# Last attention rows of the sample kept in SBUF, and three more PSUM banks for the last output products

## The chip, the cores and the metric

The kernel runs on one core of a Trainium2 chip. The metric is the time of one execution on the device in microseconds (us); lower is better. Three runs of the kernel before gave a median of 1077.6 us (1075.97 to 1082.05). One further execution was profiled; its time and its span stand in the table below.

The core has a matrix engine (TensorE, PE in the profile; its weight loads are the row PEld), a vector engine (VectorE, DVE), an activation engine (ScalarE, ACT), a general engine (GpSimd, POOL) and SyncE (SP), on whose queue this kernel issues all its DMAs. SBUF is the on-chip memory that the engines read, PSUM the eight banks into which PE writes its products, and DRAM is off the chip.

## The reference, cut to what matters

One encoder layer is applied to a prompt of 1024 tokens and, with the same weights, to a sample of 512 tokens, 1024 channels each:

```
h = rmsnorm(x, norm_g);  z = h @ w_in
y_hy  = rmsnorm(x0 * long_conv(x1 * vv), on_hy) * silu(hy_gate)             # 512 channels
y_att = rmsnorm(neighbourhood_attention(q, k, v, rpb), on_att) * silu(att_gate)  # 512 channels
y     = x + concat([y_hy, y_att]) @ w_out                                   # 1024 -> 1024
```

Attention has 8 heads of 64 channels, so two heads fill 128 partitions; the kernel calls such two heads a pair, and the 512 attention channels are the four pairs 0 to 3. The RMS norm over all 512 attention channels needs the sum of squares of all four pairs.

## The kernel before, in words

Matrix products are done in split single precision. Each operand is a rounded part `hi` and a remainder `lo`, and a product is three matmuls: hi by hi, weight-lo by hi, weight-hi by lo.

The kernel is written as generators (`k_phase`, `hyena`, `attention`, `out_part`), which `weave` steps through in a planned order; the compiler's planner then orders the instructions of each engine, earlier program text first, some generators with a higher priority. Each engine works through its own instructions strictly in the order so fixed. A tile from a pool with a tag shares a fixed number of buffers with the other tiles of that tag; a new tile waits until an old one is released by its last reader.

**Attention of the sample** (`attention(Gs, ap)`, lines 877 to 1065). For each pair it loads q, k, v and a bias table, makes scores and softmax (`soft`, tag `sp`, two PSUM banks), and then the product with v (`values`, tag `tp`, three PSUM banks): two transposed blocks, each copied and split by ACT (line 1012) and DVE (line 1013), then a bank with the product, which ACT and DVE add into the SBUF tile `ya` (lines 1023, 1024). When a pair is done, `finish` (lines 1026 to 1037) squares `ya` (ACT), adds the squares into `sqs` (POOL), for the last pair starts the sum over channels on PE (`row_sum`, line 811), multiplies `ya` by the gate (DVE, line 1036, in the profile line 76), and writes it to the DRAM buffer `A_d`. `row_r` then makes the 1/RMS factor `ra_s` in fourteen small DVE instructions.

**Output** (`out_part`, lines 1068 to 1103). Part 0 is the hyena half of `w_out`, part 1 the attention half; a job is 512 tokens (two of the prompt, one of the sample). For its four blocks of 128 channels a job loads `A_d` into the tile `lo` (line 1078), ACT rounds it into `hi` (line 1079) and POOL subtracts (line 1080). Then, for each half h of the 1024 output columns and each t of four blocks of 128 tokens, one PSUM bank collects twelve matmuls: three for each block k of channels, in the order k = 0, 1, 2, 3. DVE scales the bank, adds it to `acc` (line 1100), and SP writes the result out (line 1102). In part 1 of the sample there are thus eight products P1 to P8 of twelve matmuls, 96 in all; block k is pair k, so the last three matmuls of every product need pair 3, and the scaling needs `ra_s`.

**Banks.** In this phase PSUM is divided into tags `mm` (2 banks), `mo` (1), `sp` (2) and `tp` (3). The products of the output take their banks from a fixed list (line 1209), which for P1 to P8 comes out as mm, mm, mo, mm, mm, mo, mm, mm. So three products can be open at a time.

The prompt's products and the sample's attention are woven together (line 1221); the sample's part 1 follows (line 1222).

Of the kernel before, what the change touches and what calls it, by code (L numbers as in the profile page):

```python
# [23 lines left out]
NB = 4  # L24
# [10 lines left out]
def f32(ap):  # L35
    return ap.bitcast(F32)


class Group:
    def __init__(self, name, L, x, out, z2, dec, tw0):  # L40
        self.name, self.L, self.x, self.out, self.z2, self.dec = name, L, x, out, z2, dec
        self.nt = L // P
        self.xs, self.hi, self.lo = [], [], []
        self.rows = L // GW
        self.B = 2 * L // P
        self.half = self.B // 2
        self.tw0 = tw0
        self.nseg = L // 512


class Kernel:
# [825 lines left out]
    def attention(self, G, ap):  # L877
        nc, v = self.nc, self.v
        L, nt, rows = G.L, G.nt, G.rows
        big = G.name == "p"  # L880
# [145 lines left out]
        def finish(pr, s, y):  # L1026
            sl = slice(s * 512, (s + 1) * 512)
            sq = sqs[:, sl] if pr == 0 else ap.tile([P, 512], F32, name="qkr", bufs=2)
            nc.scalar.activation(out=sq, in_=y, func=AF.Square)
            if pr:  # L1030
                self.add(sqs[:, sl], sqs[:, sl], sq, nc.gpsimd)
            if pr == NB - 1 and s == G.nseg - 1:
                self.row_sum(ssa, sqs, "sp")
            ga = ap.tile([P, 512], F32, name="qkr", bufs=2)
            self.dma(ga, self.ga_d[G.name][pr][:, sl])
            self.stt(y, y, v["on_att"][:, pr:pr + 1], ga, ALU.mult)
            self.dma(self.A_d[G.name][4 + pr][:, sl], y)

        pair, todo = load_pair(0)
        for f in todo:  # L1040
# [3 lines left out]
        for pr in range(NB):  # L1044
            nxt, todo = load_pair(pr + 1) if pr + 1 < NB else (None, [])
            for e in range(2):
                Vh = load_head(pr * 2 + e)
                for hf in range(2):
                    for unit in units:
                        ss = soft(pair, e, hf, unit)  # L1050
                        late = [(n - 1, f) for n, f in late]
                        for n, f in late:
                            if n == 0:
                                f()
                        late = [x for x in late if x[0] > 0]
                        late.append((1, lambda a=(pair, Vh, e, hf, unit, ss): values(*a)))
                        if e == 1 and hf == 1:
                            late.append((2, lambda a=(pr, unit[0], pair[3][unit[0]]): finish(*a)))
                        if e == 1 and todo:
                            todo.pop(0)()  # L1060
                        yield
            pair = nxt
# [5 lines left out]
    def out_part(self, part, jobs):  # L1068


        nc = self.nc
        for jb in jobs:
            G, sl = jb["G"], slice(jb["seg"] * 512, (jb["seg"] + 1) * 512)
            jb["hi"] = [jb["ops"].tile([P, 512], F32R, name=f"hi{k}") for k in range(4)]
            jb["lo"] = [jb["ops"].tile([P, 512], F32R, name=f"lo{k}") for k in range(4)]
            for k, (hi, lo) in enumerate(zip(jb["hi"], jb["lo"])):
                a = f32(lo)
                self.dma(a, self.A_d[G.name][part * 4 + k][:, sl])
                nc.scalar.copy(out=hi, in_=a)  # L1079
                self.sub(lo, a, f32(hi), nc.gpsimd)  # L1080
            if part == 0:
                jb["acc"] = jb["accs"].tile([P, 4, D], F32, name="acc")
        yield
        for h in range(2):
            hs = slice(h * 512, (h + 1) * 512)
            units = [self.take_w(("w_out", h, part, k // 2)) for k in range(4)]
            for jb in jobs:
                G, t0, acc = jb["G"], jb["seg"] * 4, jb["acc"]
                r = G.ratt if part else G.rhy
                if part == 0:  # L1090
                    self.dma(acc[:, :, hs], G.x[t0 * P:(t0 + 4) * P, hs].rearrange("(t p) c -> p t c", p=P))
                for t in range(4):
                    ps = self.bank(next(self.mm_tags))
                    tok = slice(t * P, (t + 1) * P)
                    for k, (whi, wlo) in enumerate(units):
                        hi, lo = jb["hi"][k][:, tok], jb["lo"][k][:, tok]
                        for i, (w, a) in enumerate(((whi, hi), (wlo, hi), (whi, lo))):
                            nc.tensor.matmul(ps, lhsT=a, rhs=w, start=(k == 0 and i == 0), stop=(k == 3 and i == 2))  # L1098
                    o = acc[:, t, hs]
                    self.stt(o, ps, r[:, t0 + t:t0 + t + 1], o)  # L1100
                    if part == 1:
                        self.dma(G.out[(t0 + t) * P:(t0 + t + 1) * P, hs], o)
                yield
# [11 lines left out]
    def run(self):  # L1115
# [16 lines left out]
        def cls(*cms):  # L1132
            for cm in cms:
                cm.__exit__(None, None, None)
# [84 lines left out]

        self.w_pools, self.w_bufs = itertools.cycle((wp, self.wp)), 8  # L1220
        self.weave(self.chain(self.out_part(0, jobs), self.out_part(1, jobs[:2])), self.attention(Gs, ap))
        self.weave(self.out_part(1, jobs[2:]))
        cls(wc, *cms[::-1], ac)
        self.psum("right")
# [149 lines left out]
```

## Time and profile before

| | |
|---|---|
| median of three runs | 1077.6 us |
| profiled execution, its own time | 1074.62 us |
| its span (first to last instruction) | 1072.8 us |
| granted clock of PE, mean over the span | 0.975 |
| PE busy | 996.7 us, 93% |
| DVE busy | 788.4 us, 73% |
| ACT busy | 455.0 us, 42% |
| POOL busy | 394.9 us, 37% |

The busy shares are means over stages with different limits. A granted clock of 1.00 is 2.4 GHz, of 0.50 is 1.2 GHz. Matmuls overlap, so the length of one is longer than the distance from its start to the next one's.

### The profile page before, as it was taken

Reading aid. Unit: us, or ns where it says so; the run is one execution under the profiler, and the core shown is the slowest. Engines: PE = TensorE matmul, PEld = TensorE weight load, DVE = VectorE, ACT = ScalarE, POOL = GpSimd, SP = SyncE. Lnnn points to the kernel's source line nnn. Section 1 sums busy time; section 2 is a strip of 40 time slices with the busy share of each in tenths; the row PEclk is TensorE's granted clock in tenths of the full one; section 3 lists DMA queues with packets and bytes.
Section 4 is the critical chain, followed back from the end, with each engine's and each line's share of the span. In section 5 each row is a group of like instructions: output and inputs, shape, how many; then the busy total and the mean of one; then the engine's idle time right before and its main releaser. Section 6 shows DMA issues by size and latency. Waiting matters only on the chain.

```text
span 1072.8 us, 16738 instructions
## 1 busy us (share of the span) xinstructions
PE 996.7 (93%) x5868; PEld 877.5 (82%) x5868; DVE 788.4 (73%) x2036; ACT 455.0 (42%) x942; POOL 394.9 (37%) x318
## 2 busy tenths in 40 slices
PE   3899899998999999999998999998999989999976
PEld 2889798887888888888886887888988878888765
DVE  5797949455148676977648999989878867867863
ACT  6543423332332322222216465565756652465530
POOL 1043221302133332424155534445355365654540
PEclk9999899999999999999999999999999989999998
DMA  8217261664721121211394343654654479445422
GB/s 304 70 40 232 100 222 62 211 209 143 249 65 52 69 67 55 82 39 64 111 302 119 104 116 105 174 138 130 182 152 126 122 245 307 139 142 161 132 92 98
DMA packets 105778, 148.46 MB, mean 138 GB/s; under 512 B 7665, under 2 KB 69947, under 8 KB 105183
## 3 DMA queue, kind: packets, MB, share of 16 engines
q1 hardware_dynamic: 105695, 147.40, 43.9%
q8 instruction: 46, 0.75, 0.3%
q14 instruction: 37, 0.30, 0.1%
HBM read 106.15 MB, written 41.22 MB: 137 GB/s over the span
## 4 chain that ended last, share of the span: by engine, by line
PE 59%; DVE 20%; DMA 11%; ACT 4%; issue 3%; SPq 1%; POOL 1%; DVEq 0%; ACTq 0%; POOLq 0%
PE bank L398 28%; PE bank L1098 9%; PE bank L411 4%; PE bank L450 4%; DMA dec<-in_dec_p_dram 3%; PE bank L1019 2%; PE bank L452 2%; PE bank L451 2%; PE bank L1010 2%; DVE zc L64 1%; DVE s_sb L988 1%; SPq L61 1%; DVE whi L371 1%; DMA K_s<-Kw 1%; DVE xk L64 1%
## 5 line engine op out<-in xcount | busy, mean ns | idle before, releaser
L64 POOL TENSOR_TENSOR wlo<-wraw,whi 128x512 fp32r<-128x512 f32 x150 | 222.0, 1486 | 483.9 <-ACT whi L371 341.3
L398 PE MATMUL bank<-hThi_p,whi 128*128 128x512 f32 x320 | 126.8, 396 | 3.8 <-DVE vg L64 3.8
L398 PE MATMUL bank<-hThi_p,wlo 128*128 128x512 f32 x320 | 126.8, 396 | 0.0
L398 PE MATMUL bank<-hTlo_p,whi 128*128 128x512 f32 x320 | 126.4, 395 | 0.0
L411 PE MATMUL bank<-whi,hThi_p 128*128 128x256 f32 x384 | 110.8, 290 | 4.9 <-ACT qsq L832 2.4
L411 PE MATMUL bank<-whi,hTlo_p 128*128 128x256 f32 x384 | 109.7, 291 | 0.0
L411 PE MATMUL bank<-wlo,hThi_p 128*128 128x256 f32 x384 | 109.3, 286 | 0.0
L992 ACT ACTIVATE s_sb<-s_sb,mx 128x360 f32<-128x360 f32 (+1 forms) x96 | 60.4, 630 | 75.7 <-DVE mx L988 74.9
L1098 PE MATMUL bank<-whi,hi 128*128 128x512 f32 x192 | 78.4, 410 | 6.4 <-ACT hi L1079 4.6
L411 PEld LDWEIGHTS bank<-whi,hThi_p 128*128 128x128 f32 x384 | 74.0, 193 | 7.1 <-ACT qsq L832 2.6
L1098 PE MATMUL bank<-wlo,hi 128*128 128x512 f32 x192 | 77.3, 403 | 0.0
L1098 PE MATMUL bank<-whi,lo 128*128 128x512 f32 x192 | 76.8, 404 | 0.0
L371 ACT CAST whi<-wraw 128x512 fp32r<-128x512 f32 x66 | 40.5, 620 | 81.5 <-PE bank L398 69.5
L411 PEld LDWEIGHTS bank<-wlo,hThi_p 128*128 128x128 f32 x384 | 74.1, 193 | 0.5 <-issue 0.5
L411 PEld LDWEIGHTS bank<-whi,hTlo_p 128*128 128x128 f32 x384 | 73.3, 193 | 0.5 <-issue 0.5
L398 PEld LDWEIGHTS bank<-hThi_p,whi 128*128 128x128 f32 x320 | 60.6, 189 | 15.9 <-DVE vg L64 4.0
L1019 PE MATMUL bank<-pt,V 120*64 120x256 f32 (+1 forms) x352 | 67.7, 299 | 4.5 <-DVE pt L64 2.5
L398 PEld LDWEIGHTS bank<-hThi_p,wlo 128*128 128x128 f32 x320 | 60.6, 189 | 12.1
L398 PEld LDWEIGHTS bank<-hTlo_p,whi 128*128 128x128 f32 x320 | 60.4, 189 | 12.0
L398 PE MATMUL bank<-hThi_s,whi 128*128 128x512 f32 x160 | 64.1, 403 | 3.8 <-ACT vg L832 3.2
L64 POOL TENSOR_TENSOR T<-cmask,qkr 128x480 f32<-128x480 f32 x32 | 39.5, 1242 | 67.4 <-DMA qkr<-in_rpb_dram 49.2
L64 DVE TENSOR_TENSOR pt<-bank,pt 120x384 fp32r<-120x384 f32 (+1 forms) x96 | 56.1, 595 | 11.0 <-ACT pt L1012 10.3
(276 smaller groups left out, 2692.9 us busy)
## 6 DMA issues: line engine op xcount, KB each, us to landing
wraw<-in_w_ch_dram SPq DMA_DIRECT2D x40, 512.0 KB
wraw<-in_w_tk_dram SPq DMA_DIRECT2D x24, 512.0 KB
V<-v_p SPq DMA_DIRECT2D x32, 240.0 KB
wraw<-in_w_out_dram SPq DMA_DIRECT2D x24, 256.0 KB
out_dram<-acc SPq DMA_DIRECT2D x24, 256.0 KB
v_p<-vg SPq DMA_DIRECT2D x32, 160.0 KB
K_p<-Kw SPq DMA_DIRECT2D x4, 1088.0 KB
x<-in_x_prompt_dram SPq DMA_DIRECT2D x8, 512.0 KB
```

Source lines behind the costliest of these rows:

```text
L61: eng.dma_start(out=out, in_=in_)
L64: (eng or self.nc.vector).tensor_tensor(out=out, in0=a, in1=b, op=op)
L371: next(self.w_round)(out=hi, in_=r)
L398: nc.tensor.matmul(ps, lhsT=w, rhs=h[s][:, k], start=(k == 0 and i == 0), stop=(k == KC - 1 and i == 2))
L411: nc.tensor.matmul(pss[t // 2][:, t % 2, :], lhsT=h[t // 4][:, k, t % 4 * P:(t % 4 + 1) * P], rhs=w, start=(k == 0 and i == 0 and t % 2 == ...
L450: mm(o, lhsT=c, rhs=z, start=True, stop=False)
L451: mm(o[:, 0:P], lhsT=ns if inverse else s, rhs=z[:, 1], start=False, stop=False)
L452: mm(o[:, P:], lhsT=s if inverse else ns, rhs=z[:, 0], start=False, stop=True)
L992: nc.scalar.activation(out=s_sb[:, :n], in_=s_sb[:, :n], func=AF.Exp, bias=mx, scale=-1.0, accum_out=l)
L1010: nc.tensor.transpose(out=tp_[0:120, c * P:(c + 1) * P], in_=s_sb[:, c * 120:(c + 1) * 120], identity=self.ident)
L1019: nc.tensor.matmul(o, lhsT=vl, rhs=pr_, start=(c == 0 and i == 0), stop=(c == ncu - 1 and i == 1))
L1098: nc.tensor.matmul(ps, lhsT=a, rhs=w, start=(k == 0 and i == 0), stop=(k == 3 and i == 2))
```

## The change

`finish` keeps the gated `ya` of the sample's last pair as `G.last` and does not write it to `A_d`. `out_part` makes `hi` and `lo` of the fourth block straight from that tile; the subtraction for this block runs on DVE (the default of `sub`), where POOL did it. And ahead of the sample's part 1 a new list of tags is set.

```diff
@@ Group.__init__
-        self.xs, self.hi, self.lo = [], [], []
+        self.xs, self.hi, self.lo, self.last = [], [], [], None
@@ attention / finish
-            self.dma(self.A_d[G.name][4 + pr][:, sl], y)
+            if pr == NB - 1 and not big:
+                G.last = y
+            else:
+                self.dma(self.A_d[G.name][4 + pr][:, sl], y)
@@ out_part
             for k, (hi, lo) in enumerate(zip(jb["hi"], jb["lo"])):
+                if part == 1 and k == 3 and G.last is not None:
+                    nc.scalar.copy(out=hi, in_=G.last)
+                    self.sub(lo, G.last, f32(hi))
+                    continue
@@ run
         self.weave(self.chain(self.out_part(0, jobs), self.out_part(1, jobs[:2])), self.attention(Gs, ap))
+        self.mm_tags = itertools.cycle(["mm", "mm", "mo", "tp", "tp", "tp"])
         self.weave(self.out_part(1, jobs[2:]))
```

P1 to P8 then take mm, mm, mo, tp, tp, tp, mm, mm: six banks before the first has to be used again.

## Rows read from the trace of the kernel before

**Rows 1.** The page's part 2: PE's busy tenths and the DMA rate in 40 slices.
```profile
PE   3899899998999999999998999998999989999976
...
GB/s 304 70 40 232 100 222 62 211 209 143 249 65 52 69 67 55 82 39 64 111 302 119 104 116 105 174 138 130 182 152 126 122 245 307 139 142 161 132 92 98
```

**Rows 2.** Chain of waits from 1000 us on: start us, length us, what (line).
```profile
1040.38 0.49 ACT pt L1012
...
1040.90 0.57 DVE pt L64
...
1041.51 0.81 PE bank L1019 x5
...
1042.34 0.37 ACT ya L1023
...
1042.74 0.44 DVE ya L64
...
1043.86 1.86 DVE ya L76
...
1045.74 1.99 DMA A_s<-ya
...
1047.75 2.55 DMA lo<-A_s
...
1050.33 0.62 ACT hi L1079
...
1051.00 3.36 PE bank L1098 x7
...
1054.38 0.76 DVE acc L76
...
1055.19 13.91 PE bank L1098 x60
...
1069.12 0.75 DVE acc L76
```

**Rows 3.** Busy time per stretch of the end: length, five engines (instructions), clock, DMA, GB/s.
```profile
1037.60:1042.30 4.70, 3.16 (x19) 2.15 (x18) 2.99 (x6) 1.32 (x3) 0.00 (x0) 1.00 0.01 3
1042.30:1051.00 8.70, 1.88 (x10) 1.79 (x9) 4.58 (x16) 1.61 (x3) 1.26 (x1) 0.60 0.20 60
1051.00:1055.20 4.20, 3.82 (x10) 2.71 (x10) 0.82 (x2) 0.00 (x0) 1.27 (x1) 0.62 0.00 0
1055.20:1069.10 13.90, 13.88 (x60) 11.17 (x60) 4.25 (x6) 0.00 (x0) 0.00 (x0) 1.00 0.36 132
1069.10:1072.80 3.70, 0.00 (x0) 0.00 (x0) 0.75 (x1) 0.00 (x0) 0.00 (x0) 0.79 0.19 71
```

**Rows 4.** The same view for one microsecond, where the clock fell.
```profile
1044.00:1045.00 1.00, 0.00 (x0) 0.00 (x0) 1.00 (x1) 0.00 (x0) 1.00 (x1) 0.50 0.00 0
```

**Rows 5.** PE in order of time: start, length, line, operation, count, idle before.
```profile
1037.25 0.39 PE L1098 MATMUL bank<-whi,lo 128*128 128x512 f32 x1
...
1039.80 0.49 PE L1010 MATMUL bank<-ident,s_sb 128*120 128x128 f32 x3
...
1045.22 1.87 PE L811 MATMUL bank<-ones,sqs 128*128 128x1 f32 x8 [2.92 <-POOL sqs L64]
```

**Rows 6.** POOL in order of time.
```profile
1031.60 5.78 POOL L64 TENSOR_TENSOR wlo<-wraw,whi 128x512 fp32r<-128x512 f32 x4
1043.90 1.26 POOL L64 TENSOR_TENSOR sqs<-sqs,qkr 128x512 f32<-128x512 f32 x1 [6.52 <-ACT qkr L1029]
1051.02 1.27 POOL L64 TENSOR_TENSOR lo<-lo,hi 128x512 fp32r<-128x512 f32 x1 [5.85 <-ACT hi L1079]
```

**Rows 7.** ACT in order of time: rounding of pair 2.
```profile
1029.07 0.62 ACT L1079 CAST hi<-lo 128x512 fp32r<-128x512 f32 x1 [0.41 <-DMA lo<-A_s]
```

**Rows 8.** DVE in order of time: the gate product of pair 2, the last step of `ra_s`.
```profile
1019.80 0.74 DVE L76 SCALAR_TENSOR_TENSOR ya<-ya,pc,qkr 128x512 f32<-128x512 f32 x1
...
1049.70 0.17 DVE L816 COPY ra_s<-rs_y 128x4 f32<-128x4 f32 x1
```

## The prediction

> **What bounds the kernel now.** I read the page's slices first: PE is busy nine tenths in nearly every slice, but only seven and six tenths in the last two [rows 1]. A loss that the mean of 93% hides sits at the very end. Next comes the chain of waits backwards from the last instruction [rows 2]. It shows the last output bank scaled at 1069.12, before it 60 matmuls of line 1098 without a hole, and before these a string in which PE does almost nothing: pair 3's last values are added into `ya`, gated, written to DRAM (1.99 us), read back (2.55), rounded by ACT (0.62), and only then multiplied. The stretches put a size on it [rows 3]. From 1037.6 to 1042.3 PE works 3.16 of 4.7 us on the last values; from 1042.3 to 1051.0 it works 1.88 of 8.7; from 1051.0 to 1055.2 it runs at a mean clock of 0.62; from 1055.2 on it is full.
>
> How much work waits there? Sixty matmuls start from 1055.19 [rows 2]: five whole products of twelve. So the first three products were open, each with the nine matmuls of k = 0 to 2 done (27, the last of them at 1037.25 [rows 5]) and the three of pair 3 missing, which are the nine matmuls of 1051.0 to 1055.2. That P4 did not go on at 1037.6 is a matter of banks: its k = 0 to 2 need `hi` of pair 2, rounded at 1029.07 [rows 7], and weights, whose last remainder was there at 1037.4 [rows 6]. Two limits therefore stand one behind the other, the way of pair 3 through DRAM and three open products; the change goes at both.
>
> **The change part by part.** All times are of the profiled execution (1074.62 us, span 1072.8), which is 3.0 us under the median of 1077.6; I carry the difference over to the median.
>
> *The way through DRAM.* The write and the read go, with the small issue gaps between: `ya` was final at 1045.72 (1043.86 + 1.86), the rounding began at 1050.33 [rows 2]. Now ACT, idle at that time, can begin at about 1045.74 and `hi` is there at 1046.4 instead of 1050.95: 4.6 us earlier. On SP's queue nothing stood behind these two issues but the output DMAs, which start after 1055, so the queue gives nothing else.
>
> *The remainder on DVE.* It was POOL's, 1.27 us [rows 6], and becomes a 128x512 DVE instruction with two SBUF inputs. Nearest rows: the gate product of pair 2 took 0.74 [rows 8], that of pair 3 took 1.86 [rows 2], beside POOL's addition from 1043.90 to 1045.16 [rows 6]. The new one would start at 1046.4, when POOL has nothing left, so I take 0.75 and keep 1.9 as the other end: `lo` at 1047.1 to 1048.3. Behind it on DVE stand the fourteen small instructions of `ra_s`, which ended at 1049.87 [rows 8] and now end up to 0.75 later, at 1050.6; who needs `ra_s` comes below.
>
> The page "SBUF — State Buffer" of the Trainium skill, section "Who interferes with whom", says that a DVE instruction with two SBUF inputs contends with a GpSimd instruction that reads SBUF. The 0.74 against 1.86 agrees. By that rule the move to DVE would cost the change its 1.1 us again if POOL were reading at 1046.4.
>
> *The banks.* The three `tp` banks serve the last `values`: one is free when the last block but one has been split, the next when the last has (1041.47), the third when `ya` has been added (1043.18) [rows 2]. So P4 can open at about 1041, P5 at 1041.5, P6 at 1043.2: 27 matmuls that PE can do while it waited. Price of one: 13.91 us for 60, 0.23 us [rows 2], so 6.2 us. I credit none of them to the holes before 1042.3, though P4 may find up to 0.7 us there.
>
> *The sum.* From 1042.3: 27 matmuls of k = 0 to 2, 6.2 us; in between the eight of `row_sum`, 1.87 us at the low clock they had [rows 5], 0.9 if at the full one; together to 1050.4 at the latest. By then `hi` and `lo` of pair 3 have been there for 2 us or more, so PE doesn't wait for them. Then the 18 last matmuls of P1 to P6, 4.1 us, to 1054.5; then P7 and P8, 24 matmuls, 5.5 us, to 1060.0. P7 needs a bank back, so P1 scaled: `ra_s` at 1050.6 plus 0.75 is 1051.4; if `row_sum` stands behind all 27, `ra_s` comes at 1050.4 + 2.8 + 0.75 = 1053.9, P1 is free at 1054.7, and P7 waits 0.2. PE's end was 1069.1, so 9.1 us are saved with every term at its dear end. With `row_sum` at the full clock (0.9) and P4 in the holes (0.7) it is 10.7. I take 9.5. The stretch behind PE's end, 3.7 us for the last scaling and its DMA [rows 3], stays: the eight output DMAs, 256 KB each, now follow each other in some 9 us, 233 GB/s, and slices of the page reach 304 and 307 [rows 1].
>
> Of these 9.5 us, some 1.6 come from the clock: 4.2 us at a mean of 0.62 [rows 3] hold 3.2 us at half speed, 1.6 us lost. PE before had next to no work between 1042.3 and 1051.0, and the clock was down to 0.50 by 1044 [rows 4]. With PE filled from 1041 I expect it to stay at 1.00.
>
> **The rivals.**
>
> *Clock down all the same.* For it: PE works only 3.16 of the 4.7 us before 1042.3 and part of this is transposes. Against it: throughout that stretch the clock was 1.00 [rows 3], and the fall came after 1.7 us with nothing at all. Price: one low stretch like that of 1051.0, 1.6 us, up to 3.2 if `row_sum` and the products are hit twice. Saved 6.3 to 7.9, so 1069.7 to 1071.3.
> The page "TensorE: Matmul & The Clock Gate" of the Trainium skill, section "Part 4: PE-mode transpose", says that transposes do not count as PE busy in the same way; by that rule the stretch to 1042.3 looks emptier to the gate than to the profile. The trace's 1.00 there doesn't bear it out so far.
>
> *Banks without use.* PE's order is fixed by the planner from its own durations. If it takes the gate product for 0.74 where the chip needs 1.86 [rows 2, 8], it may place the k = 3 matmuls, or `row_sum`, ahead of P5 and P6; PE then stands before a ready product. In the limit only the DRAM way counts: everything as before but 4.6 us earlier, 1073.0. For it: the planner let PE take k = 3 as soon as it saw `hi`. Against it: by program order and readiness 27 matmuls need 6.2 us, more than the 4.1 from 1042.3 to 1046.4, so at most P6 can fall behind, and costs a stall of about 1.5 us, which the range holds.
>
> *Slower: attention loses its banks.* P4 to P6 now draw on the tag that attention itself needs. P4 lacks only pair 2 long before the end, so the planner could open it, and at 1030 to 1037 also P5, in `tp` banks that then stay taken until pair 3 arrives. Attention would go through one bank: two blocks of 0.49 + 0.49 + 0.57 each, then about 0.8 + 0.4 + 0.4 for the product, 4.7 us a unit with nothing overlapped [rows 2, 5]. It decides from two units on (9.4 us, the whole gain); at three it is 1077.6 - 9.5 + 14.1 = 1082. Against it: attention has the higher priority, and PE was never without prompt products before 1037, so P4 would not have been called for.
>
> **How the numbers follow.** My forecast, 1077.6 - 9.5 = 1068, has a chance of 0.63 with its own range of 1065 to 1071 (the bounds 10.7 and 9.1, a stall of 1.5 and a little for the spread of the runs). More gain than that, because P4 and P5 fill holes before 1042: 0.06, about 1064. Clock down: 0.11, 1070.5. Banks without use: 0.14, 1073. Attention slowed: 0.06, 1082. The range from 1063 to 1074.5 leaves out the last and the tails. A measurement of this kernel tells 0.5% from no change, 5.4 us: faster means below 1072.2. The forecast, the greater gain and the clock case lie there, and a few of the third: 0.80. Same takes the rest of the third, 0.14; slower 0.06.
>
> **What would show it.** No DMA from `ya` and no read of A_s after the last gate product; ACT's rounding within 0.1 us behind it; some 27 matmuls of line 1098 between 1041 and 1050; a granted clock of 1.00 there; PE's last matmul near 1060 and one unbroken stretch of some 42 matmuls ahead of it; a span of about 1063. The step on banks is wrong if PE is still idle for more than 2 us between 1043 and the rounding's end; the forecast is wrong if the last values of attention end later than 1043.2, or if anything before 1037 has moved.

## The result and the profile after

The changed kernel has a median of 1065.79 us (1062.47 to 1069.32, four runs) beside 1078.01 us of the kernel before (1075.97 to 1082.05, four runs): ratio 0.9883, 95% interval 0.9838 to 0.9927. It is 12.2 us faster by the medians; 1068 was forecast. The profiled execution took 1062.47 us, its span is 1060.7 us. On another occasion the same kernel gave a ratio of 0.9916 (0.9891 to 0.9942); the two intervals overlap between 0.9891 and 0.9927.

Single runs of one kernel lie up to 15 us apart, and much of that arises ahead of the change. The last of the 27 matmuls that the first three products do without pair 3 started at 1037.25 in the trace before [rows 5], at 1035.73 in the one after, and at 1042.55 in a second trace of the same changed kernel; these last two executions are 6.8 us apart there and 6.8 us apart in their whole time. Up to that matmul PE's instructions stand in the same order in all traces of this document. So the traces are compared from its start on, which I call the *reference point*, and the time from there to the end of the span the *last stretch*: 1072.8 - 1037.25 = 35.55 us before, 1060.7 - 1035.73 = 24.97 after, 24.95 in the second trace. The change is worth 10.6 us by this measure. The kernel before was traced once; two kernels below that were traced twice differ between their traces by 0.3 and 2.5 us in the last stretch.

PE's slices on the page after: the last two now hold nine and eight tenths, where they held seven and six [rows 1].
```profile
span 1060.7 us, 16734 instructions
...
PE   3999899888999999999998898999999989999998
```
The chain of waits after, columns as in [rows 2]:
```profile
1037.72 0.74 PE bank L1019 x5
...
1039.41 0.39 PE bank L1019
1039.80 2.06 PE bank L1105 x9
1041.85 0.58 PE bank L1019 x5
1042.43 4.11 PE bank L1105 x18
1046.54 0.79 PE bank L811 x8
1047.33 9.70 PE bank L1105 x42
...
1057.05 0.75 DVE acc L76
```
Line 1105 is the old line 1098 (1102 or 1106 in some kernels below), and 1081 the rounding of the old line 1079 for pair 3. Before, this chain ran from `ya` over two DMAs and ACT to seven and then sixty matmuls [rows 2]. Now it doesn't leave PE from 1039.41 to 1057.03: nine matmuls of P4, the last value products, eighteen of P5 and P6, `row_sum`, then the 42 that were still to come. No DMA and no ACT is in it. Stretch by stretch (columns as in [rows 3]):
```profile
1036.10:1039.40 3.30, 1.98 (x13) 1.39 (x12) 2.44 (x6) 1.32 (x3) 0.00 (x0) 1.00 0.04 12
1039.40:1046.40 7.00, 6.99 (x34) 5.85 (x35) 2.86 (x3) 1.49 (x3) 1.29 (x1) 1.00 0.00 0
1046.40:1057.10 10.70, 10.61 (x51) 8.51 (x49) 7.75 (x23) 0.13 (x1) 0.00 (x0) 1.00 0.46 172
1057.10:1060.70 3.60, 0.00 (x0) 0.00 (x0) 0.70 (x1) 0.00 (x0) 0.00 (x0) 0.83 0.20 73
```
PE is busy 17.6 of 17.7 us at a clock of 1.00, where it had stretches at 0.60 and 0.62 [rows 3]. What is left at the end is the last scaling and its DMA, 3.6 us, as before.

PE in order of time, columns as in [rows 5]:
```profile
1035.73 0.39 PE L1105 MATMUL bank<-whi,lo 128*128 128x512 f32 x1
...
1042.27 0.40 PE L1105 MATMUL bank<-whi,hi 128*128 128x512 f32 x1
...
1046.38 0.95 PE L811 MATMUL bank<-ones,sqs 128*128 128x1 f32 x8
1047.19 0.49 PE L1105 MATMUL bank<-whi,hi 128*128 128x512 f32 x1
...
1050.05 1.52 PE L1105 MATMUL bank<-whi,lo 128*128 128x512 f32 x6
```
`row_sum` takes 0.95 us where it took 1.87 at the low clock. The first matmul with pair 3 is at 1047.19, the first with its remainder at 1050.05.

DVE after, in order of time: gate product, the new remainder, the end of `ra_s`.
```profile
1043.99 1.88 DVE L76 SCALAR_TENSOR_TENSOR ya<-ya,pc,qkr 128x512 f32<-128x512 f32 x1 [0.70 <-ACT qkr L1029]
1046.57 0.69 DVE L64 TENSOR_TENSOR lo<-ya,hi 128x512 fp32r<-128x512 f32 x1 [0.69 <-ACT hi L1081]
...
1049.95 0.17 DVE L816 COPY ra_s<-rs_y 128x4 f32<-128x4 f32 x1
```
ACT after, its last instruction:
```profile
1045.91 0.62 ACT L1081 CAST hi<-ya 128x512 fp32r<-128x512 f32 x1 [1.95 <-DVE ya L76]
```
The rounding follows the gate product (1045.87) after 0.04 us. It ends at 1046.53; PE wants it at 1047.19. That is a slack of 0.66 us, and it matters below.

### The profile page after: what moved, and what is told of

Same layout as the page of the kernel before. It is cut to its first block, busy times and chain, and to the rows that moved or that the text cites. A ratio compares the mean times of both kernels' runs of the same rounds, so it can differ in the third digit from the quotient of the medians.

```text
span 1060.7 us, 16734 instructions
## 1 busy us (share of the span) xinstructions
PE 991.3 (93%) x5868; PEld 871.3 (82%) x5868; DVE 788.5 (74%) x2037; ACT 455.1 (43%) x942; POOL 392.8 (37%) x317
## 4 chain that ended last, share of the span: by engine, by line
PE 53%; DVE 25%; DMA 11%; ACT 5%; issue 3%; SPq 2%; POOL 1%; DVEq 0%; ACTq 0%; POOLq 0%
PE bank L398 25%; PE bank L1105 6%; PE bank L411 5%; PE bank L450 4%; PE bank L1019 2%; PE bank L452 2%; PE bank L451 2%; SPq L61 2%; DVE whi L371 2%; PE bank L1010 2%; DVE s_sb L988 2%; DVE zc L64 2%; DMA dec<-in_dec_p_dram 1%; DMA v_p<-vg 1%; DVE s L64 1%
```

## The experiments

The theory: PE's work is the bound of the last stretch, and both parts of the change close the same standstill, the banks from the front (more work to do in it), SBUF from the back (a shorter wait). The rivals: only one of the two counts. The diffs are against the changed kernel; three products are open at a time in the kernel before, six in the changed one. Stretches are in us.

| kernel | open | pair 3 | last stretch | ratio to before (95%) |
|---|---|---|---|---|
| before | 3 | DRAM | 35.55 | 1 |
| SBUF alone | 3 | SBUF | 31.61, 31.94 | 0.9990 (0.9964 to 1.0016), 0.9952 (0.9929 to 0.9975) |
| four open | 4 | SBUF | 32.79, 30.28 | 0.9950 (0.9932 to 0.9969) |
| five open | 5 | SBUF | 27.08 | 0.9913 (0.9883 to 0.9943) |
| the change | 6 | SBUF | 24.97, 24.95 | 0.9883 (0.9838 to 0.9927), 0.9916 (0.9891 to 0.9942) |
| seven open | 7 | SBUF | 25.26 | 0.9906 (0.9881 to 0.9931) |
| remainder on POOL | 6 | SBUF | 24.94 | 0.9896 (0.9872 to 0.9920) |
| banks alone | 6 | DRAM | 31.26 | 0.9958 (0.9939 to 0.9977) |
| seven open, DRAM | 7 | DRAM | 27.69 | 0.9920 (0.9891 to 0.9949) |
| banks alone, eight idle matmuls | 6 | DRAM | 31.81 | 0.9967 (0.9937 to 0.9997) |
| banks alone, four idle matmuls | 6 | DRAM | 29.02 | 0.9957 (0.9932 to 0.9983) |

**The change once more**, as a mark for the others.

> The changed kernel once more, as the mark for the others. My theory (PE is filled from the last values of attention to the end, so neither DRAM nor banks are left in the way): about 12 us under the kernel before, PE without a hole over 0.3 us from the fourth product's first matmul on, last stretch (from the last matmul of the third product's first nine to the end of the span) 25.0 us against 35.6 before. Rival, the gain was partly a lucky draw of the runs: under 8 us faster this time, with the same last stretch.

The median is 1065.46 us against 1074.62 for the kernel before: 9.2 faster, between my 12 and the rival's 8. The stretch of 24.95 repeats to 0.02 us; the medians do not, so I take 12 us for partly a draw of the runs, and 10.6 for the better figure.

**Banks alone.**
```diff
-            if pr == NB - 1 and not big:
-                G.last = y
-            else:
-                self.dma(self.A_d[G.name][4 + pr][:, sl], y)
+            self.dma(self.A_d[G.name][4 + pr][:, sl], y)
```


> Six banks, but pair 3 goes through DRAM as before. My theory (the two parts cover the same wait): 27 matmuls are done in the wait, then PE stands still for 3.9 us until pair 3 is rounded; last stretch 28.9 us if the clock stays up, 30.5 if it falls; 5 to 6.6 us faster than before. Rival 'banks do it all': last stretch 25.0, equal to the change. Rival 'the DRAM way does it all': last stretch about 35, no gain.

31.26: neither rival, and 0.8 above the 30.5 that I gave for a fallen clock. PE in order of time around the standstill:
```profile
1051.25 0.95 PE L811 MATMUL bank<-ones,sqs 128*128 128x1 f32 x8
1056.11 0.79 PE L1102 MATMUL bank<-whi,hi 128*128 128x512 f32 x1 [3.91 <-ACT hi L1083]
1056.70 0.63 PE L1102 MATMUL bank<-wlo,hi 128*128 128x512 f32 x1
1057.13 0.63 PE L1102 MATMUL bank<-whi,hi 128*128 128x512 f32 x1
```
and the same kernel by stretches:
```profile
1052.20:1056.10 3.90, 0.00 (x0) 0.00 (x0) 2.30 (x14) 0.62 (x1) 0.00 (x0) 0.73 0.26 75
1056.10:1060.00 3.90, 3.89 (x9) 3.12 (x10) 0.00 (x0) 0.00 (x0) 1.27 (x1) 0.50 0.00 0
1060.00:1061.00 1.00, 1.00 (x4) 0.77 (x4) 0.00 (x0) 0.00 (x0) 0.00 (x0) 0.59 0.00 0
1061.00:1068.00 7.00, 7.00 (x32) 5.49 (x30) 4.71 (x7) 0.00 (x0) 0.00 (x0) 1.00 0.71 261
```
All work up to `row_sum` is as in the changed kernel, then PE stands for 3.91 us as expected, and the matmuls behind it start 0.43 us apart at a clock of 0.50. The stretch is 6.3 us longer than the change's: 3.9 of standing, and 2.4 more that I put down to the clock here and tested below.

**SBUF alone**, run twice.
```diff
-        self.mm_tags = itertools.cycle(["mm", "mm", "mo", "tp", "tp", "tp"])
```


> Pair 3 stays in SBUF, tags as before (three products open). My theory: rounding 4.6 us earlier, nothing else, the clock still falls; last stretch 31.0 us, 4.6 us faster than before (29.4 if the clock stays up). Rival 'the DRAM way does it all': last stretch 25, 10 us faster. Rival 'banks do it all': 35.

Stretch by stretch:
```profile
1049.10:1053.20 4.10, 1.19 (x7) 1.16 (x6) 2.28 (x2) 1.61 (x3) 1.26 (x1) 0.81 0.00 0
1053.20:1058.00 4.80, 4.80 (x14) 3.41 (x13) 3.85 (x17) 0.00 (x0) 0.00 (x0) 0.50 0.00 0
1058.00:1072.10 14.10, 14.07 (x60) 11.34 (x60) 4.21 (x6) 0.00 (x0) 0.00 (x0) 0.98 0.35 130
```
The stretch is 3.9 us shorter. The wait of 8.7 us in [rows 3] is down to 4.1, but the clock falls all the same and the sixty matmuls at the end are the same sixty. The median time, however, hardly moved, so it was run again.

> Pair 3 in SBUF with three products open, once more: the last stretch was 3.9 us shorter than before, but the time hardly differed (ratio 0.999). My theory (a draw of the runs; everything ahead of the last stretch is the same code in the same order): last stretch 31.6 us again, or 30 where the clock falls later, and about 4 us faster than before. Rival 'the time is given back ahead of the stretch': ratio 0.999 again.

Ratio 0.9952, stretch 31.94: the same program, 5.0 us by the medians this time and 0 the first. So this time nothing was given back ahead of the stretch. That the first time was a draw of the runs is likely but not shown; if so, a single median of this kernel can be some 4 us off even with twelve runs. In this second trace the clock fell earlier, already under attention's last value products:
```profile
1041.30:1042.30 1.00, 0.37 (x4) 0.13 (x2) 0.87 (x3) 0.84 (x2) 0.00 (x0) 1.00 0.00 0
1042.40:1044.20 1.80, 1.62 (x6) 1.03 (x5) 0.35 (x1) 0.03 (x1) 0.00 (x0) 0.50 0.00 0
```

**More and fewer open products.** Seven with pair 3 in SBUF:
```diff
-        self.mm_tags = itertools.cycle(["mm", "mm", "mo", "tp", "tp", "tp"])
+        self.mm_tags = itertools.cycle(["mm", "mm", "mo", "sp", "tp", "tp", "tp", "mm"])
```


> The change with a seventh bank (the fourth product takes one of the two sp banks, the seventh product the last tp bank). My theory (PE already full): nothing, last stretch 25.0 us, within 0.3. Rival 'open products are still the limit': 2 us less for nine more matmuls in the wait, 23.0.

By stretches, the two that hold PE's work:
```profile
1041.00:1048.00 7.00, 7.00 (x35) 5.85 (x35) 2.84 (x3) 1.49 (x3) 1.29 (x1) 1.00 0.00 0
1048.00:1058.70 10.70, 10.60 (x51) 8.56 (x49) 7.59 (x22) 0.12 (x1) 0.00 (x0) 1.00 0.29 105
```
PE was full with six banks and is full now, for the same length to the tenth; a seventh bank has nothing to fill. The stretch is 0.3 us longer, and that lies behind PE's last matmul. The same list with pair 3 through DRAM:

> Seven banks and pair 3 through DRAM. My theory: 36 matmuls in the wait instead of 27, so the standstill for pair 3 shrinks from 3.9 to 1.9 us; last stretch 26.9 us. Rival 'DRAM costs its 4.6 us whatever PE has to do': 29.6.

```profile
1056.32 0.40 PE L1102 MATMUL bank<-whi,lo 128*128 128x512 f32 x1
1058.32 0.50 PE L1102 MATMUL bank<-whi,hi 128*128 128x512 f32 x1 [1.60 <-ACT hi L1083]
```
Nine more matmuls shorten the standstill from 3.91 to 1.60 us, and the clock stays at 1.00 behind it: stretch 27.69, 3.6 us shorter than with six banks, more than the 2.05 us of nine matmuls. So what DRAM costs depends on what PE has left to do. It is 0.8 us above my 26.9, and about that much lies behind PE: all products are finished late, and DVE scales the eight in one row,
```profile
1062.06 5.36 DVE L76 SCALAR_TENSOR_TENSOR acc<-bank,ra_s,acc 128x512 f32<-128x512 f32 x8 [4.76 <-PE bank L1102]
```
so that the span ends 4.5 us after PE's last matmul (1066.10). With the change it is 3.7 us, with seven banks and SBUF 4.0.

Four and five open (the first new line is four, the second five):
```diff
-        self.mm_tags = itertools.cycle(["mm", "mm", "mo", "tp", "tp", "tp"])
+        self.mm_tags = itertools.cycle(["mm", "mm", "mo", "tp", "mm", "mm", "mo", "mm"])
+        self.mm_tags = itertools.cycle(["mm", "mm", "mo", "tp", "tp"])
```


> Pair 3 in SBUF, five products open. My theory: PE stands 1.2 us; last stretch 26.2 us, clock at 1.00. Rival 'the number of banks does not matter once pair 3 is in SBUF': 25.0.

27.08 instead of 26.2: the trend is right and the size short. PE's waits:
```profile
1047.73 1.05 PE L811 MATMUL bank<-ones,sqs 128*128 128x1 f32 x8 [0.86 <-POOL sqs L64]
1048.93 0.50 PE L1105 MATMUL bank<-whi,hi 128*128 128x512 f32 x1
...
1052.96 0.50 PE L1105 MATMUL bank<-whi,hi 128*128 128x512 f32 x1 [0.33 <-DVE acc L76]
```
From start to start PE loses 1.0 us ahead of `row_sum` (0.86 of it idle) and 0.4 behind it, where pair 3's rounding ends only at 1048.88; that is the standstill that I had in mind, 1.4 us instead of 1.2. Another 0.5 (0.33 of it idle) is a wait that I had not counted: for a bank to come back, whose scaling waits for `ra_s`, ready at 1052.04. That is 1.9 of the 2.1 us beside the change, with the clock at 1.00.

> Pair 3 in SBUF, four products open (one tp bank). My theory: each open product is nine matmuls, 2.05 us, of the wait; PE stands 3.2 us between the last values and pair 3; last stretch 28.2 us, 29.8 if the clock falls. Rival 'the number of banks does not matter once pair 3 is in SBUF': 25.0.

32.79, slower than with three products open. The stretch that did it holds P4's nine matmuls:
```profile
1042.20:1046.10 3.90, 3.86 (x10) 3.07 (x11) 0.56 (x1) 0.00 (x0) 0.00 (x0) 0.56 0.00 0
```
The clock fell as P4 began, behind the first of attention's last value products, and a second time behind the next hole (2.92 us, ahead of `row_sum`); since P4's matmuls stand ahead of the other value products in PE's order, `ya` came later too. The same kernel again:

> Four products open, once more, for the clock: in the first run it fell to 0.50 already under the fourth product's first nine matmuls. My theory (the level there is at the edge, since PE has only the last values of attention between the third and the fourth product): it may or may not fall this time; last stretch 30.5 us without, 32.8 with. Rival 'four products are slower for another reason': 32.8 with the clock at 1.00 there.

```profile
1039.00:1042.00 3.00, 2.92 (x15) 2.40 (x15) 0.56 (x1) 0.03 (x1) 0.00 (x0) 1.00 0.00 0
...
1046.20:1050.00 3.80, 3.75 (x10) 2.96 (x11) 2.75 (x15) 0.00 (x0) 0.00 (x0) 0.58 0.00 0
```
This time the clock held under P4 and fell once, behind that hole: 30.28. Two executions of one program with the same holes, 2.5 us apart by the clock.

**The remainder on POOL.**
```diff
-                    self.sub(lo, G.last, f32(hi))
+                    self.sub(lo, G.last, f32(hi), nc.gpsimd)
```


> The change, but the remainder of pair 3 is subtracted on POOL as before. My theory: it is done at about 1.3 us after the rounding instead of 0.7, still before PE's first use of it 2.8 us later; last stretch 25.0, and ra_s 0.7 us earlier, which nobody waits for. Rival 'the remainder stands on the path': 25.6.

POOL and PE of that run, in order of time:
```profile
1050.73 1.29 POOL L64 TENSOR_TENSOR lo<-ya,hi 128x512 fp32r<-128x512 f32 x1 [1.28 <-ACT hi L1081]
```
```profile
1054.18 1.53 PE L1105 MATMUL bank<-whi,lo 128*128 128x512 f32 x6
```
Ready at 1052.02, wanted at 1054.18; 24.94. The choice of engine is worth nothing here. That `ra_s` would come 0.7 us earlier was wrong: it ended 14.6 us behind the reference point, and 14.4 with the change. It waits for `row_sum` (until 11.6 in both), and the remainder on DVE was done before that (11.5).

**Idle matmuls in the standstill**, to price the clock by itself. To the kernel with banks alone, matmuls into the spare `sp` bank are added behind `row_sum`, eight in the first kernel and four in the second; nobody reads them.
```diff
                 self.row_sum(ssa, sqs, "sp")
+                if not big:
+                    idle = self.bank("sp")
+                    for _ in range(8):
+                        nc.tensor.matmul(idle, lhsT=sqs[:, 0:P], rhs=sqs, start=True, stop=True)
```


> The kernel with six banks and pair 3 through DRAM, and eight matmuls into a spare bank behind row_sum that nobody reads (single precision, 128x512, about 0.43 us each, 3.4 us in all), where PE stood still for 3.9 us and the clock then was at 0.50 for the 18 last matmuls of the first six products. My theory (of the 6.3 us that the DRAM way costs beside six banks, 3.9 are the standstill and 2.4 the low clock): the standstill is filled and thus lost either way, the clock stays at 1.00, last stretch 28.9 us instead of 31.3. Rival 'the slow matmuls wait for something else (the remainder on POOL)': 31.3 with the clock at 1.00; or the extra work costs its 3.4 us: 34.7.

The first try missed, since each of these products shows as two records, 0.44 us from one to the next:
```profile
1051.63 7.11 PE L1037 MATMUL bank<-sqs 128*128 128x512 f32 x16
1058.18 0.79 PE L1106 MATMUL bank<-whi,hi 128*128 128x512 f32 x1
```
They ran 2.5 us beyond the rounding (done at 1055.67 there), and the clock was at 1.00: 31.81, as much as with standing and slow clock. With four:

> As the run before with its eight idle matmuls, but four: the eight took 7.1 us (each in two passes of 0.44) and overran the standstill of 3.9 us by 2.9. My theory (six banks with the DRAM way lose 3.9 us to the standstill and 2.4 to the low clock behind it): four take 3.5 us, end before pair 3 is rounded, the clock stays at 1.00, last stretch 28.9 us against 31.3 without them. Rival 'the 2.4 us are the wait for POOL's remainder, not the clock': 31.3 with the clock at 1.00.

```profile
1055.53 3.68 PE L1037 MATMUL bank<-sqs 128*128 128x512 f32 x8
1059.36 0.50 PE L1106 MATMUL bank<-whi,hi 128*128 128x512 f32 x1
```
and by stretch:
```profile
1059.30:1069.20 9.90, 9.84 (x42) 7.75 (x42) 4.70 (x7) 0.01 (x1) 1.29 (x1) 1.00 0.47 174
```
The 42 matmuls behind the wait in the chains of the two kernels, without idle matmuls and with four:
```profile
1056.11 12.01 PE bank L1102 x42
```
```profile
1059.36 9.85 PE bank L1106 x42
```
The same work takes 2.2 us less, and the stretch is 29.02 against 31.26, with PE doing more and not less. POOL's remainder is as late as without them (begun 15.4 us behind the reference point, 15.5 without). So 2.2 of the 6.3 us are the clock, and 4.1 are the standstill. The medians can't show such a step: the ratios are 0.9958 and 0.9957. The page "TensorE: Matmul & The Clock Gate" of the Trainium skill, section "What's actually happening", says that a throttled state is the default and activity releases it; this pair of runs agrees: the same kernel at 0.50 behind 3.9 us of nothing, and at 1.00 behind 3.7 us of matmuls without use.

No version clearly beats the change: with seven banks the median is 1064.76 us beside 1065.46 on the same occasion, too near to tell apart, and the stretch is 0.3 us longer.

## Why the prediction was right

**What bounds the end** was read rightly. Before, 27 matmuls could be done ahead of pair 3; 27 more fit into the wait, and PE is now the bound from 1039.4 on. Both one-sided rivals fell with the two half changes, and the experiments with four to seven banks show the wait being filled nine matmuls at a time.

**DRAM way, 4.6 us.** Shown alone it is just that: rounding ended 13.70 us after the reference point before [rows 2, 5] and 9.10 after it with SBUF alone. In the full change it came at 10.80, only 2.9 us earlier, because the planner put all nine matmuls of P4 between the first and the other five of the last value products. These ended at 5.06 us behind the reference point before and at 6.70 after. That P4 "can open at about 1041" came true (3.90 us behind the point); what stands behind it in PE's order I had not counted, although every product there was on the list. The sign I had given against the forecast, last values later than 1043.2, thus did occur by this measure (7.57 us behind the point; the limit is 5.95). It did no harm because the bound had moved to PE, but the 2 us of slack that I gave to pair 3 were 0.66. That this was enough is partly luck, since the delay was not in the sum.

**Sum.** The terms were right and the credit was mis-sized, within its own bounds. I settled at 9.5 between 9.1 and 10.7; PE's end came 10.55 us earlier (31.83 us behind the point before, 21.28 after), near the upper bound. `row_sum` took 0.95 us, the cheap end of 0.9 to 1.87. P4's nine matmuls take 2.06 us in the chain and put off the end of the last values by 1.64, so the holes gave 0.4 of the 0 to 0.7 us that I allowed. And P7's wait of 0.2 us did not come; I had left it out of the 9.1, whose dear end is 8.9 with it. The other 1.6 us of the measured 12.2 lie within the scatter of the medians: the repetition gave 9.2.

**Remainder on DVE**: 0.69 us, beside POOL at rest; the gate product again 1.88 us beside POOL's addition. `ra_s` ended 14.4 us behind the reference point, 12.6 before, and no product waited for it.

**Clock.** It stayed at 1.00 as forecast. The rival was real, and its 0.11 about fair. PE's order up to P4 is the same in all eleven traces with four or more products open, and in one of them (four open, the first) the clock fell as P4 began. With SBUF alone it fell in the same place in one of two traces, 3.8 us behind the reference point. The Trainium skill's remark on transposes (page "TensorE: Matmul & The Clock Gate", section "Part 4: PE-mode transpose") is neither shown nor refuted: the stretch before the fall holds transposes, value products and holes alike, and the clock was at 1.00 throughout it.

**Banks without use, attention slowed**: neither occurred. P5 and P6 were ahead of the k = 3 matmuls in PE's order, and `tp` banks were taken only after attention's last blocks had theirs.

## What to carry to other kernels

When a late operand meets an accumulation with many early ones, count how much of the accumulation can be done without it, and how many banks that takes. Here hiding the wait (banks alone, 4.3 us) and shortening it (SBUF alone, 3.6 to 3.9 us) were worth about the same. Each alone left a part of the wait and, behind it, a low clock; the two together left neither and saved 10.6 us, more than the sum of both. Once PE is full, a further bank gains nothing: with seven the scalings at the very end only stand closer together. Compare such changes from a common point in the traces where the runs scatter by more than the gain.

## What was not expected

- A standstill of 3.91 us cost another 2.2 us through the clock; one of 1.60 us cost none (six and seven banks with DRAM).
- Two executions of the kernel with four open products differ by 2.5 us in the last stretch, through the clock alone falling earlier in one.
- A single-precision matmul 128x512 shows as two records and took about 0.9 us (7.11 us for eight), against 0.23 us from start to start for one of the kernel's own, whose operands are rounded.
